# An encoder block on one core: the first phase's matmuls grouped by weight part, and the scalar work of the last product reordered

## The chip, the cores and the metric

The kernel runs on one core of a Trainium2 chip, in one launch. The metric is the device time in microseconds (us) of that core. The table of times has three runs of the kernel before, and one execution of it was also taken with the hardware profiler; its rows are what the prediction quotes. In those rows PE is the matmul engine, PEld its weight loads, DVE the vector engine, ACT the scalar engine, POOL the GpSimd engine, SP the engine that issues most transfers; a q behind an engine (ACTq, SPq) marks what its queue does, such as issuing a DMA. L324 is line 324 of the kernel before.

## The reference, cut to what matters

One encoder layer over 256 tokens of width 2048 in float32: a root-mean-square norm, one combined input projection, windowed and dilated attention, two gated branch projections, an output projection, a gated MLP with a convolution, and a gated per-token embedding, then a final norm. The change touches the first columns of the input projection and the very end:

```
h = rms_norm(x, attn_norm[i])
proj = h @ w_in[i]
...
gate_p = jax.nn.sigmoid(rms_norm(x, ple_norm[i]) @ w_ple_gate[i])
x = x + gate_p * (p[i] @ w_ple_proj[i])
...
return rms_norm(x, final_norm)
```

## The kernel before, in words

**Weights.** All weights come as one stream of 128x128 blocks in the order in which PE uses them (`_stream`). Blocks are loaded in tiles `raw` (six buffers, on SP's queue), mostly eight blocks each. `split_to` turns each such group, called a sub here, into a high part `whi` (ACT, L261) and a low part `wlo` (DVE, L262, which reads `whi`); both names have four buffers. The features are held in the same way: `hs` (named `mov` in the profile) has the high part of a feature chunk in its first 256 columns and the low part in the next 256. A product is high part times both halves (512 columns) plus low part times the first half (256 columns).

**The first phase.** Seven products (`FIRST = 7`, two keys and five queries of the windowed attention) run side by side while x and the weights arrive, for each of 16 feature chunks one block of each product, so 112 blocks. Their sums stand in seven banks (`firsts`, three named acc, two sp, two pt). The first piece of 16 blocks is cut in subs of 1, 2, 5, 4 and 4 blocks, and then each sub has eight: subs 0 to 16 belong to the first phase. The loop before emits, for each block, one matmul of the high part and at once one of the low part, in `block` (L324 and L325), as far as features and subs are there (`ready`, `_SUBS`).

**Between first phase and attention.** Two matmuls make the table of attention biases (L616, into the one-buffer bank `misc`), which DVE adds to the mask (`rows`, L618) and SP writes out. `tot` holds the squares of x summed over chunks; four calls sum it over partitions (L488, each shown as two matmuls, into `misc` again), DVE makes `rv` of it (L500), POOL raises it to the power -1/2 (L502), DVE writes it on diagonals (`rdg`, L510), and a matmul spreads it (L516, `misc` again). Each `first` is gathered from its bank by ACT (L464, tile t, two buffers) and DVE (L468, L470). Then comes the product of the values (L375 to L377, two acc banks), and after it the products of single heads (`eight`, L347 and L350), in which the high parts of eight blocks stand in a row and then eight low parts, each second sub the other way round, so that runs of 16 meet.

**The last product.** `last_gates` finishes the gate for the last 512 columns, first for the first 128 tokens (t = 0), then for the other 128 (t = 1), for these in two halves of 256 columns: the right half (side 1, whose rest of the product PE does first) and the left one (side 0). `gate_side` is tanh (ACT, L951), plus one times `ph` (L952), added to the residual (L953), squares with their sum (L954), times the last gain (L955). `last_root` makes the norm's factor (DVE L986, POOL L987), and `finish` scales and writes 128 tokens: the last 512 columns on DVE (L994, written by SP), the first 768 on ACT (L996, written on ACT's own queue, L997), the 768 between on DVE (L998, written by SP, L999).

**What sets the order.** The code is recorded, and a scheduler sets the order on each engine; instructions wrapped in `keep` stay in the order of the code among themselves. So an edit can move instructions that its lines do not name.

## Time and profile before

| | us |
|---|---|
| median of three runs | 1464.53 |
| lowest, highest | 1463.12, 1464.62 |
| the profiled execution, its own time | 1464.53 |
| its span in the profile | 1462.7 |
| what lies around the span | 1.83 |
| mean granted PE clock in it | 0.997 |

The profile's page gives busy time of each engine, the chain of work that ended last, and groups of instructions. A row of a timeline has the start, the time taken, the engine, the line, the tile written and the tiles read, and in brackets how long the engine sat idle before it and who ended that. A row of the chain has start, length and what it was; an x with a number joins that many equal pieces.

### The profile page before, as it was taken

How to read it: one execution, taken by the hardware profiler on the slowest of the kernel's cores; microseconds unless marked ns; L12 is line 12 of the kernel's file. 1: busy time of each engine (PE TensorE's matmuls, PEld its weight loads, DVE VectorE, ACT ScalarE, POOL GpSimd, SP SyncE). 2: the span in 40 equal slices, each digit the busy share in tenths (PEclk: the TensorE clock that was granted, in tenths of full speed). 3: DMA queues.
4: the chain of work that ended last, by engine and by line, in shares of the span. 5: the costliest groups of instructions: out<-in, count | busy, mean ns of one | idle time of the engine just before them, and what ended most of it. 6: DMA issues, size and time to landing. Idle time of an engine off the chain costs nothing.

```text
span 1462.7 us, 20616 instructions
## 1 busy us (share of the span) xinstructions
PE 1449.0 (99%) x7531; PEld 1242.1 (85%) x7531; DVE 1110.8 (76%) x1575; ACT 818.1 (56%) x1155; POOL 107.1 (7%) x178
## 2 busy tenths in 40 slices
PE   9999999999999999999999999999999999999997
PEld 8888888888888888788888888888888888888886
DVE  7687665656665668879888888897888876988665
ACT  7465444444444456666555555676555555666653
POOL 0000000001111100201111100102110100010000
PEclk9999999999999999999999999999999999999998
DMA  9754555558888967978888886989788875797652
GB/s 327 242 172 154 173 166 181 188 179 263 290 308 299 353 226 259 291 236 273 266 284 268 285 291 212 286 286 313 274 283 276 299 230 167 255 300 252 212 193 90
DMA packets 111729, 362.16 MB, mean 248 GB/s; under 512 B 12804, under 2 KB 17924, under 8 KB 111500
## 3 DMA queue, kind: packets, MB, share of 16 engines
q1 hardware_dynamic: 88908, 292.80, 59.3%
q0 software_dynamic: 20560, 63.71, 14.6%
q10 hardware_dynamic: 2160, 4.33, 1.0%
q8 instruction: 59, 0.97, 0.3%
q14 instruction: 42, 0.34, 0.1%
HBM read 324.06 MB, written 27.30 MB: 240 GB/s over the span
## 4 chain that ended last, share of the span: by engine, by line
PE 95%; issue 2%; DMA 1%; DVE 1%; ACT 0%; SPq 0%; POOLq 0%; POOL 0%; DVEq 0%; ACTq 0%
PE acc L347 29%; PE acc L350 15%; PE acc L375 9%; PE acc L377 9%; PE acc L376 9%; PE acc L427 6%; PE acc L428 6%; PE acc L426 6%; PE first L324 2%; PE first L325 1%; DMA x<-row 1%; PE pt L894 1%; PE pt L701 0%; DMA raw<-in_wts 0%; PE sp L660 0%
## 5 line engine op out<-in xcount | busy, mean ns | idle before, releaser
L262 DVE TENSOR_TENSOR wlo<-raw,whi 128x1024 fp32r<-128x1024 f32 (+2 forms) x556 | 649.7, 1180 | 192.0 <-ACT whi L261 186.0
L261 ACT ACTIVATE whi<-raw 128x1024 fp32r<-128x1024 f32 (+2 forms) x556 | 562.2, 1022 | 303.5 <-PE acc L377 188.7
L347 PE MATMUL acc<-mov,whi 128*128 128x512 f32 x1840 | 441.6, 391 | 0.0
L347 PEld LDWEIGHTS acc<-mov,whi 128*128 128x128 f32 x1840 | 337.8, 188 | 65.5
L350 PEld LDWEIGHTS acc<-mov,wlo 128*128 128x128 f32 x1840 | 237.3, 191 | 9.1 <-ACT mov L480 0.2
L350 PE MATMUL acc<-mov,wlo 128*128 128x256 f32 x1840 | 242.8, 283 | 0.0
L375 PE MATMUL acc<-whi,mov 128*128 128x512 f32 (+1 forms) x504 | 193.4, 384 | 0.0
L377 PE MATMUL acc<-whi,mov 128*128 128x512 f32 (+1 forms) x504 | 193.1, 383 | 0.0
L376 PE MATMUL acc<-wlo,mov 128*128 128x512 f32 (+1 forms) x504 | 193.0, 383 | 0.0
L464 ACT ACTIVATE t<-acc 128x256 f32<-128x256 f32 x115 | 43.9, 382 | 132.6 <-PE acc L347 132.6
L375 PEld LDWEIGHTS acc<-whi,mov 128*128 128x128 f32 x504 | 95.1, 189 | 18.6 <-DVE first L468 0.5
L377 PEld LDWEIGHTS acc<-whi,mov 128*128 128x128 f32 x504 | 95.1, 189 | 18.6
L376 PEld LDWEIGHTS acc<-wlo,mov 128*128 128x128 f32 x504 | 95.1, 189 | 18.3
L468 DVE TENSOR_TENSOR u<-acc,t 128x256 f32<-128x256 f32 x100 | 42.2, 422 | 72.9 <-ACT t L464 72.1
L426 PE MATMUL acc<-whi,act 128*128 128x512 f32 x207 | 80.8, 391 | 0.2 <-ACT whi L261 0.2
L427 PE MATMUL acc<-wlo,act 128*128 128x512 f32 x207 | 80.6, 389 | 0.0
L428 PE MATMUL acc<-whi,act 128*128 128x512 f32 x207 | 80.6, 389 | 0.0
L853 POOL DMA_DIRECT2D x<-row x36 | 31.0, 878 | 376.8 <-ACT row L858 255.2
L262 DVE TENSOR_TENSOR wlo<-sums,whi 128x1024 fp32r<-128x1024 f32 x37 | 45.1, 1219 | 10.3 <-ACT whi L261 10.3
L805 ACT ACTIVATE c<-c 128x256 f32<-128x256 f32 x44 | 18.3, 417 | 57.3 <-DVE c L804 57.3
L426 PEld LDWEIGHTS acc<-whi,act 128*128 128x128 f32 x207 | 38.8, 188 | 8.8 <-ACT whi L261 0.9
L427 PEld LDWEIGHTS acc<-wlo,act 128*128 128x128 f32 x207 | 38.9, 188 | 8.5 <-DVE wlo L262 0.2
(218 smaller groups left out, 1664.5 us busy)
## 6 DMA issues: line engine op xcount, KB each, us to landing
raw<-in_wts SPq DMA_DIRECT2D x477, 512.0 KB, 5.0
sums<-kept SPq DMA_DIRECT2D x37, 512.0 KB, 5.3
sums<-in_wts POOLq DMA_DIRECT2D x23, 512.0 KB, 7.7
kept<-sums POOLq DMA_DIRECT2D x23, 512.0 KB, 4.5
raw<-in_wts SPq DMA_DIRECT2D x39, 256.0 KB, 4.8
row<-in_wts POOLq DMA_DIRECT2D x37, 256.0 KB, 8.7
x<-row POOLq DMA_DIRECT2D x36, 256.0 KB, 7.9
two<-in_wts POOLq DMA_DIRECT2D x14, 512.0 KB, 8.2
```

What stands on the lines that cost most here:

```text
L261: nc.scalar.activation(hi, src, AF.Copy)
L262: ins = nc.vector.tensor_tensor(lo, src, hi.bitcast(F32), op=ALU.subtract)
L347: nc.tensor.matmul(acc, hi[:, k, :], m, start=(first and k == 0), stop=(last and k == SUB - 1), skip_group_check=True)
L350: nc.tensor.matmul(acc[:, T:], lo[:, k, :], m[:, :T], start=False, stop=False, skip_group_check=True)
L375: nc.tensor.matmul(acc, xh, hi, start=(k == 0), stop=False)
L376: nc.tensor.matmul(acc, xh, lo, start=False, stop=False)
L377: nc.tensor.matmul(acc, xl, hi, start=False, stop=(k == n - 1 - t * late))
L426: nc.tensor.matmul(acc, xh, hi, start=(e == 1), stop=False)
L427: nc.tensor.matmul(acc, xh, lo, start=False, stop=False)
L428: nc.tensor.matmul(acc, xl, hi, start=False, stop=(e == uses[name]))
L464: keep(nc.scalar.activation(t, acc[:, T:], AF.Copy, scale=scale))
L468: nc.vector.tensor_tensor(u, acc[:, :T], t, op=ALU.add)
```

## The change

In the first phase `firsts_to` takes the place of `block`: of each stretch within a sub it emits all high parts, then all low parts, and from sub 7 on each second sub the other way round. In `last_gates` the tanh of the right half is emitted ahead of `finish(0, ...)`, that of the left half stays behind it; all of them and the copies in `finish` are under `keep`. For t = 0 the middle 768 columns are scaled by ACT in place of DVE. The two multiplications by the last gain become one of 512 columns, behind the second `last_root`.

```diff
-    def block(acc, m, first, last, ahead=3):
...
-        nc.tensor.matmul(acc, hi[:, o, :], m, start=first, stop=False, skip_group_check=True)
-        nc.tensor.matmul(acc[:, T:], lo[:, o, :], m[:, :T], start=False, stop=last, skip_group_check=True)
...
+    def firsts_to(end):
+
+        while state["at"] < end:
+            a = state["at"]
+            s, o = _SUB_OF[a]
+            b = min(end, _SUBS[s][0] + _SUBS[s][1])
+            turned = s > 6 and s % 2 == 1
+            for low in (turned, not turned):
+                for c in range(a, b):
+                    k, e = divmod(c, FIRST)
+                    w, m = subs[s][low][:, o + c - a, :], hs[:, k, :]
+                    nc.tensor.matmul(firsts[e][:, T * low:], w, m[:, :2 * T - T * low], start=(k == 0 and not low),
+                                     stop=(k == KC - 1 and low != turned), skip_group_check=True)
+            state["at"] = b
+            if b == _SUBS[s][0] + _SUBS[s][1]:
+                del subs[s]
...
-        while state["at"] < min(FIRST * ready, _SUBS[state["sub"]][0]):
-            k, e = divmod(state["at"], FIRST)
-            block(firsts[e], hs[:, k, :], k == 0, k == KC - 1, ahead=0)
+        firsts_to(min(FIRST * ready, _SUBS[state["sub"]][0]))
...
-    def gate_side(n, t, acc, u, side, total):
+    def gate_side(n, t, u, side, total):
...
-        nc.scalar.activation(u[:, c], acc, AF.Tanh, scale=held["half"][:, t:t + 1])
...
-        return lambda: keep(nc.vector.tensor_tensor(u[:, c], r, held["lg"][:, n * W4:(n + 1) * W4][:, c], op=ALU.mult))
...
         keep(nc.vector.tensor_tensor(v[:, T:], other, v[:, T:], op=ALU.add))
+        keep(nc.scalar.activation(u[:, T:], v[:, T:], AF.Tanh, scale=held["half"][:, 1:2]))
         finish(0, r, tail)
         rest()
-        u, so = row(), held["so"][:, 1:]
-        gate_side(n, 1, v[:, T:], u, 1, held["side"])()
+        gate_side(n, 1, u, 1, held["side"])
         keep(nc.vector.tensor_tensor(so, so, held["side"], op=ALU.add))
-        scaled = gate_side(n, 1, acc[1][:, :T], u, 0, held["ss3"][:, 1, n:n + 1])
+        keep(nc.scalar.activation(u[:, :T], acc[1][:, :T], AF.Tanh, scale=held["half"][:, 1:2]))
+        gate_side(n, 1, u, 0, held["ss3"][:, 1, n:n + 1])
         r = last_root(1)
-        scaled()
+        keep(nc.vector.tensor_tensor(u, res[:, 1, n * W4:(n + 1) * W4], lg, op=ALU.mult))
         finish(1, r, u)
...
-        nc.scalar.activation(whole[:, :a], whole[:, :a], AF.Copy, scale=r)
+        keep(nc.scalar.activation(whole[:, :a], whole[:, :a], AF.Copy, scale=r))
         nc.scalar.dma_start(out[t][:, :a], whole[:, :a])
-        nc.vector.tensor_scalar(whole[:, a:b], whole[:, a:b], r, None, op0=ALU.mult)
+        if t == 0:
+            keep(nc.scalar.activation(whole[:, a:b], whole[:, a:b], AF.Copy, scale=r))
+        else:
+            nc.vector.tensor_scalar(whole[:, a:b], whole[:, a:b], r, None, op0=ALU.mult)
```

Three places show what becomes of the order. An x with a number joins equal rows; line numbers above 320 are larger by a few in the changed kernel.

**End of the first phase.** On PE, the last rows of the first phase and what follows, before:

```order
L324 MATMUL first<-mov,whi 128x512
L325 MATMUL first<-mov,wlo 128x256
L616 MATMUL misc<-ohr,tbs 20x512 x2
L375 MATMUL acc<-whi,mov 128x256
L376 MATMUL acc<-wlo,mov 128x256
L377 MATMUL acc<-whi,mov 128x256
```

The same place on PE in the changed kernel:

```order
L329 MATMUL first<-mov,whi 128x512 x16
L329 MATMUL first<-mov,wlo 128x256 x16
L329 MATMUL first<-mov,whi 128x512 x16
L329 MATMUL first<-mov,wlo 128x256 x8
L619 MATMUL misc<-ohr,tbs 20x512 x2
L493 MATMUL misc<-ones,tot 128x1 x4
L380 MATMUL acc<-whi,mov 128x256
L381 MATMUL acc<-wlo,mov 128x256
```

Single pairs have become runs of 16, and the sums of `tot` (L493, L488 before) have moved up from behind the values to right behind the bias matmuls. On DVE, the same stretch before, where `rows` reads what L616 made and `rv` what L488 made:

```order
L262 TENSOR_TENSOR wlo<-raw,whi 128x1024 x3
L468 TENSOR_TENSOR first<-first,t 128x256 x2
L470 SCALAR_TENSOR_TENSOR first<-first,t 128x256
L618 TENSOR_TENSOR rows<-misc,mk 20x512
L262 TENSOR_TENSOR wlo<-raw,whi 128x1024
L470 SCALAR_TENSOR_TENSOR first<-first,t 128x256 x4
L262 TENSOR_TENSOR wlo<-raw,whi 128x1024 x4
L500 TENSOR_SCALAR rv<-misc 128x4
L510 TENSOR_SCALAR rdg<-ident,rr 128x128 x2
```

And on DVE in the changed kernel:

```order
L262 TENSOR_TENSOR wlo<-raw,whi 128x1024 x4
L621 TENSOR_TENSOR rows<-misc,mk 20x512
L473 TENSOR_TENSOR first<-first,t 128x256 x2
L505 TENSOR_SCALAR rv<-misc 128x4
L475 SCALAR_TENSOR_TENSOR first<-first,t 128x256 x2
L515 TENSOR_SCALAR rdg<-ident,rr 128x128
L475 SCALAR_TENSOR_TENSOR first<-first,t 128x256 x2
L515 TENSOR_SCALAR rdg<-ident,rr 128x128
```

`rows` now stands behind a fourth split (that of sub 20), and `rv` and `rdg` have moved up by some splits.

**End of the values.** On PE, behind the product of the values, before:

```order
L377 MATMUL acc<-whi,mov 128x256
L347 MATMUL acc<-mov,whi 128x512 x8
L350 MATMUL acc<-mov,wlo 128x256 x4
L488 MATMUL misc<-ones,tot 128x1 x4
L350 MATMUL acc<-mov,wlo 128x256 x12
L516 MATMUL misc<-rdg,ones 128x256
L347 MATMUL acc<-mov,whi 128x512 x16
```

And there in the changed kernel:

```order
L382 MATMUL acc<-whi,mov 128x256
L352 MATMUL acc<-mov,whi 128x512 x8
L355 MATMUL acc<-mov,wlo 128x256 x16
L521 MATMUL misc<-rdg,ones 128x256
L352 MATMUL acc<-mov,whi 128x512 x16
```

The sums are gone from between the low parts; the spread of `rdg` stays where it was.

**The end of the program.** On ACT, from the last square of t = 0 on, before:

```order
L884 ACTIVATE row,marks<-x 128x512
L996 ACTIVATE x<-x,rr 128x768
L951 ACTIVATE row<-row,marks 128x256
L997 DMA out<-x 128x768
L951 ACTIVATE row<-acc,marks 128x256
L996 ACTIVATE x<-x,rr 128x768
L997 DMA out<-x 128x768
```

And on ACT in the changed kernel, where L967 and L972 are the two tanh and L1001 the scaling that came from DVE:

```order
L887 ACTIVATE row,marks<-x 128x512
L967 ACTIVATE row<-row,marks 128x256
L998 ACTIVATE x<-x,rr 128x768
L999 DMA out<-x 128x768
L1001 ACTIVATE x<-x,rr 128x768
L972 ACTIVATE row<-acc,marks 128x256
L998 ACTIVATE x<-x,rr 128x768
L999 DMA out<-x 128x768
```

The right half's tanh has gone ahead of the first scaling; the write of the first tokens and one more scaling now stand ahead of the left half's tanh.

More of the change, by code (lines that the diff above doesn't have):

```diff
@@ L316, in back @@
         state["back"] = j + 1
-    def block(acc, m, first, last, ahead=3):
-        b = state["at"]
-        s, o = _SUB_OF[b]
-        split_to(s + ahead)
-        hi, lo = subs[s]
-        nc.tensor.matmul(acc, hi[:, o, :], m, start=first, stop=False, skip_group_check=True)
-        nc.tensor.matmul(acc[:, T:], lo[:, o, :], m[:, :T], start=False, stop=last, skip_group_check=True)
-        state["at"] = b + 1
-        if o == _SUBS[s][1] - 1:
-            del subs[s]
+    def firsts_to(end):
[13 more added lines that the diff above has]
+                del subs[s]
     def product(i, moving, n):
@@ L954, in gate_side @@
         keep(nc.vector.scalar_tensor_tensor(row()[:, :T], r, 1.0, r, op0=ALU.mult, op1=ALU.mult, accum_out=total))
-        return lambda: keep(nc.vector.tensor_tensor(u[:, c], r, held["lg"][:, n * W4:(n + 1) * W4][:, c], op=ALU.mult))
     def last_gates(n, acc, rest):
-        v = row()
+        v, u, so, lg = row(), row(), held["so"][:, 1:], held["lg"][:, n * W4:(n + 1) * W4]
         keep(nc.scalar.activation(v[:, T:], acc[1][:, T:], AF.Copy))
```

## The prediction, made before the changed kernel ran

> **What bounds the kernel now.** I read the page's busy times and its chain first, then who PE waited for.

> ```profile
> PE 1449.0 (99%) x7531; PEld 1242.1 (85%) x7531; DVE 1110.8 (76%) x1575; ACT 818.1 (56%) x1155; POOL 107.1 (7%) x178
> PE 95%; issue 2%; DMA 1%; DVE 1%; ACT 0%; SPq 0%; POOLq 0%; POOL 0%; DVEq 0%; ACTq 0%
> ```

> ```profile
> PE misc L516 <- DVE rdg L510: 0.4, 1, 0.4
> ```

> PE is busy for 99% of the span and makes 95% of the chain; one of its few waits is that of the spread (L516) for `rdg`. So up to PE's last matmul, what PE saves or loses moves the end one to one, and what other engines save counts only where PE waits for them. Behind that matmul a chain over ACT, DVE and POOL sets the end. The sum has a front and a tail.

> **Front, the runs.** PE's rows in the first phase, and runs of the same shapes in the later products, from the chain:

> ```profile
> 12.22 1.66 PE L324 MATMUL first<-mov,whi 128*128 128x512 f32 x6 [0.53 <-ACT whi L261]
> ...
> 45.84 0.40 PE L324 MATMUL first<-mov,whi 128*128 128x512 f32 x1
> ...
> 46.28 0.63 PE L616 MATMUL misc<-ohr,tbs 32*20 32x512 f32 x2
> 46.85 0.39 PE L375 MATMUL acc<-whi,mov 128*128 128x256 f32 x1
> ```

> ```profile
> 657.85 0.43 PE misc L516 x2
> ...
> 661.11 3.65 PE acc L347 x16
> 664.76 1.91 PE acc L350 x16
> 666.67 3.65 PE acc L347 x16
> ```

> At 12.22 PE waits for sub 5, that is for its load and its split on ACT; whatever PE saves on the 16 blocks before is lost there. From there to the last pair at 45.84 stand 95 steps of one pair: 33.62/95 = 353.9 ns a pair, with hardly a gap. In runs 16 pairs take 666.67 - 661.11 = 5.56 us, 347.5 ns a pair. The new order gives runs of 8 and 16, the same shapes; I take 347.5. Over 96 pairs PE gains 96 x 6.4 ns = 0.61 us: the first phase ends at 45.58 in place of 46.19 (45.84 and one pair). Ends of this term: no gain and 0.61; more than the runs show has no row.

> [...]

> **Front, the sums.** The order shown ahead moves the sums of `tot` from behind the values to right behind the bias matmuls. Both write `misc`, which has one buffer; so the sums can't start before DVE's `rows` has read the bias product, and the values queue behind them on PE. On DVE `rows` now stands behind the split of sub 20. The rows of before for these, ACT and then DVE:

> ```profile
> 46.48 1.05 ACT L261 ACTIVATE whi<-raw 128x1024 fp32r<-128x1024 f32 x1
> ```

> ```profile
> 44.54 1.23 DVE L262 TENSOR_TENSOR wlo<-raw,whi 128x1024 fp32r<-128x1024 f32 x1 [1.60 <-ACT whi L261]
> 45.68 0.75 DVE L468 TENSOR_TENSOR first<-first,t 128x256 f32<-128x256 f32 x2
> ...
> 46.95 0.68 DVE L618 TENSOR_TENSOR rows<-misc,mk 20x512 f32<-20x512 f32 x1
> ```

> Sub 20's high part takes the buffer of sub 16's, free when PE's last run of high parts ends. That is eight low parts, 0.96 us (half of 1.91), before the phase ends: the last high part starts at 45.58 - 0.96 - 0.23 = 44.39 and ends 0.40 later, at 44.79. Then ACT 1.05, DVE's split 1.14 until its next row (44.54 to 45.68), `rows` 0.68, and four hand-overs between engines of about 0.04 (as from ACT's tanh at 1452.34 + 0.49 to DVE's row at 1452.87, below): 44.79 + 1.05 + 1.14 + 0.68 + 0.16 = 47.82. PE would have been free at 45.58 + 0.09 + 0.57 = 46.24 (46.19 to 46.28 and on to 46.85). So PE waits some 1.58 us. The sums then cost what they cost later before, and free what was there:

> ```profile
> 60.78 0.97 PE L488 MATMUL misc<-ones,tot 128*128 128x1 f32 x8
> 61.62 1.68 PE L350 MATMUL acc<-mov,wlo 128*128 128x256 f32 x12
> 63.72 0.67 PE L516 MATMUL misc<-rdg,ones 128*128 128x256 f32 x2 [0.42 <-DVE rdg L510]
> 64.04 4.02 PE L347 MATMUL acc<-mov,whi 128*128 128x512 f32 x16
> ```

> The sums hold PE for 0.84 (60.78 to 61.62), so the values start at 47.82 + 0.84 = 48.66 in place of 46.85: 1.81 late. Their banks are free by then: the two L473 behind `rows` take 0.75. The 0.84 is gone at 60.78. And the spread no longer waits: 12 low parts from 61.62 take 1.43, so PE was through at 63.05; alone the spread holds PE for 0.43 (row at 657.85), where it went on at 64.04, so 0.99 becomes 0.43: 0.56 saved. `rdg` is now made right behind the sums, with the whole product of the values between it and its matmul. Front: 1.81 - 0.84 - 0.56 = **+0.41 us**, the 0.61 of the runs included. Next in line are the scores, which waited for nothing before; their chain from the spread is the same, so nothing new is late. SP's bias write hangs on `rows`, which ends at nearly the same time as before (47.63 against 47.8). Ends of the wait: none at all (the front is then -0.61 - 0.56 = -1.17), or ACT's split starting only when the phase has ended, 0.96 later (+1.37). I take the value between, as each of its steps has a row.

> **Tail.** DVE, then ACT with one older case of a DMA issued from its queue, POOL, and PE's last row:

> ```profile
> 1449.85 0.69 DVE L944 TENSOR_TENSOR row<-x,end 128x512 f32<-128x512 f32 x1
> ...
> 1450.69 0.42 DVE L965 TENSOR_TENSOR row<-acc,row 128x256 f32<-128x256 f32 x1
> 1451.50 0.49 DVE L994 TENSOR_SCALAR row<-row,rr 128x512 f32<-128x512 f32 x1 [0.40 <-POOL rr L987]
> 1451.90 0.61 DVE L998 TENSOR_SCALAR x<-x,rr 128x768 f32<-128x768 f32 x1
> 1452.87 0.43 DVE L952 SCALAR_TENSOR_TENSOR row<-row,end 128x256 f32<-128x256 f32 x1 [0.35 <-ACT row L951]
> ...
> 1454.55 0.42 DVE L952 SCALAR_TENSOR_TENSOR row<-row,end 128x256 f32<-128x256 f32 x1
> ...
> 1455.92 0.16 DVE L986 TENSOR_TENSOR rv<-marks,sum 128x1 f32<-128x1 f32 x1
> 1456.00 0.42 DVE L955 TENSOR_TENSOR row<-x,end 128x256 f32<-128x256 f32 x1
> ```

> ```profile
> 1451.50 0.94 ACT L996 ACTIVATE x<-x,rr 128x768 f32<-128x768 f32 x1 [0.92 <-POOL rr L987]
> 1452.34 0.49 ACT L951 ACTIVATE row<-row,marks 128x256 f32<-128x256 f32 x1
> 1452.47 0.38 ACTq L997 DMA_DIRECT2D out<-x  x1
> 1453.43 0.47 ACT L951 ACTIVATE row<-acc,marks 128x256 f32<-128x256 f32 x1 [0.59 <-PE acc L399]
> ```

> ```profile
> 1236.20 0.33 ACTq L1064 DMA_DIRECT2D pr<-in_pt  x1
> 1236.63 0.63 ACT L261 ACTIVATE whi<-raw 128x512 fp32r<-128x512 f32 x1
> ```

> ```profile
> 1450.91 0.55 POOL L987 TENSOR_TENSOR rr<-rv,mhalf 128x1 f32<-128x1 f32 x1 [93.40 <-DVE rv L986]
> 1456.23 0.60 POOL L987 TENSOR_TENSOR rr<-rv,mhalf 128x1 f32<-128x1 f32 x1 [4.76 <-DVE rv L986]
> ```

> ```profile
> 1453.11 0.28 PE L399 MATMUL acc<-whi,mov 128*128 128x256 f32 x1
> ```

> In times of before: the right half's input is there at 1451.11 (L965), so its tanh runs on ACT from 1451.15, in the time in which ACT sat idle for POOL, and ends at 1451.64. The scaling of 768 columns can follow 0.40 to 0.45 after the tanh's start, at about 1451.55, 0.05 later than before. DVE has its 512 columns at 1451.50 and, without L998, starts the right half at 1451.90, not 1452.87: 0.97 earlier. But this is only half of the tail: the left half's first DVE row (1454.55 before) needs the left tanh, which now stands on ACT behind the first write and the moved scaling. The write is issued once the scaling is done: 1451.55 + 0.94 + 0.03 = 1452.52, and holds ACT's queue for 0.38, to 1452.90; an instruction behind such an issue started 0.10 after it (1236.53 to 1236.63), so the moved scaling runs from 1453.00, the tanh 0.84 behind it (as 1451.50 to 1452.34), from 1453.84 to 1454.31, and DVE goes on at 1454.35. PE's last matmul ends at 1453.39, so the tanh no longer waits for PE; ACT takes PE's place. DVE is ready earlier, at about 1453.3 (four steps of 0.46 from 1451.90, since the multiplication L955 is gone there). So the tail gains 1454.55 - 1454.35 = **0.20 us**, not 0.97. Were ACT not held by the issue, the tanh would again start at 1453.43 and the gain be 0.61; these are the ends.

> From 1454.35 on everything follows as before, but for the multiplication, now 512 columns (0.69, as L944) behind `rv`, where 256 stood (0.42). It runs while POOL makes the factor: `rv` to the end of POOL is 0.91 (1455.92 to 1456.83), `rv` and the multiplication 0.77, so it is hidden. If that cover fails, 0.27 (rival below). The middle write of the first tokens follows the moved scaling's end at 1453.94, not L998's at 1452.51:

> ```profile
> out<-x SPq DMA_DIRECT2D x2, 384.0 KB, 3.1
> ```

> At 1453.94 + 3.1 = 1457.04 it has landed before the last writes are issued (POOL's end, 1456.83 - 0.20, and a scaling of 0.61: 1457.24), so it costs nothing; without that cover it would share the engines with them for at most its delay of 1.43.

> **Sum.** +0.41 - 0.20 = +0.21 on the profiled execution's own 1464.53 (span 1462.7 and 1.83 around it): 1464.74, say 1464.7. The median of the three runs is the same 1464.53.

> **Rivals.**
> 1. *POOL is held by the multiplication.* L955 reads two SBUF tiles while POOL works; beside it POOL took 0.60, beside L965, which reads a bank and one tile, 0.55. If POOL has to wait until the longer multiplication ends, the factor comes 0.69 - 0.42 = 0.27 later: +0.48, 1465.0. For it: the 0.05. Against it: POOL started 0.19 before L955 ended and wasn't longer by that. [...]
> 2. *ACT isn't held by the issue*: -0.61 in the tail, +0.41 in front, -0.20: 1464.3. Against it: the 0.10 at 1236.53, and that the issue itself waits for the scaling.
> 3. *PE doesn't wait for `rows`*: -1.17 - 0.20 = -1.37, 1463.2. Against it: one buffer for both products.
> 4. *The change doesn't do what it says*: runs at the pace of pairs, +0.21 + 0.61 = +0.82, 1465.35. [...]
> 5. *Slower: the low runs starve.* A run of low parts of two subs takes 1.91 us, and needs the second sub's split at its start plus 0.96. Sub 9, in the first stretch that DVE filled with other work, has it from 20.24:

> ```profile
> 20.24 1.22 DVE L262 TENSOR_TENSOR wlo<-raw,whi 128x1024 fp32r<-128x1024 f32 x1
> ```

> It is there at 21.46; PE would want it at about 23.3 (12.22, four high runs of 1.83 and four low ones of 0.96). Slack 1.9 us: from a DVE that is later by more than that, each of the five such runs waits for up to one split, 5 x 1.23 = 6.15: 1470.9. Against it: the slack, and that later subs come earlier against their use.

> **How the numbers follow.** Chances: forecast 0.49, rival 1 0.22, rival 2 0.12, rival 3 0.08, rival 4 0.05, rival 5 0.03, and 0.01 for a gain that I don't see. All but the last two lie within 0.2% (2.9 us, about what a measurement of this kernel can tell from no change) of 1464.53: faster 0.01, same 0.96, slower 0.03. Range: the cases but rival 5 span 1463.2 to 1465.35; the later split adds up to 0.96 to the forecast (1465.7), and the runs of before lay up to 1.4 under their median. 1463.0 to 1466.0 holds them.

> **What would show it.** Right: the bias matmuls about 0.6 us earlier; a PE wait of about 1.6 us at the sums, put down to `rows`; no wait at the spread; the first head product behind the spread about 0.4 us later than 64.04; in the tail the left tanh some 0.4 us after PE's last matmul, right behind the moved scaling; POOL still about 0.6. Wrong: new PE waits for `wlo` between 12 and 46, POOL near 0.9, or other waits of PE after 80 us, where the orders are alike again.

## The result, and the profile after

| | kernel before | changed kernel |
|---|---|---|
| median, us (22 runs each) | 1464.32 | 1466.22 |
| lowest to highest, us | 1462.98 to 1465.65 | 1463.62 to 1468.92 |
| the profiled execution, us | 1464.53 | 1463.65 |
| its span, us | 1462.7 | 1461.9 |

The ratio is 1.0013, with an interval of 1.0007 to 1.0019: the changed kernel is 1.9 us slower, 0.22 us above the top of the range that was predicted. Yet the execution of it that was profiled is at the low end of its runs, below the median of the kernel before. A profile is one execution, and here that one lacks what most of the others have. So this section reads what every execution shares, and the experiments find the rest. One run of the changed kernel in those experiments took 3637.75 us, at full clock and for a reason that no record shows; it counts in the first median of their first table, but in no ratio.

PE of the changed kernel around the end of the first phase:

```profile
11.74 2.12 PE L329 MATMUL first<-mov,whi 128*128 128x512 f32 x8 [0.20 <-ACT whi L261]
...
44.32 1.11 PE L329 MATMUL first<-mov,wlo 128*128 128x256 f32 x8
45.36 0.63 PE L619 MATMUL misc<-ohr,tbs 32*20 32x512 f32 x2
47.48 1.08 PE L493 MATMUL misc<-ones,tot 128*128 128x1 f32 x8 [1.48 <-DVE rows L621]
48.42 0.36 PE L380 MATMUL acc<-whi,mov 128*128 128x256 f32 x1
...
63.77 0.59 PE L521 MATMUL misc<-rdg,ones 128*128 128x256 f32 x2
64.01 4.01 PE L352 MATMUL acc<-mov,whi 128*128 128x512 f32 x16
```

PE idles 1.48 us for `rows`, as forecast (1.58), and no longer waits at the spread. Sub 5 starts at 11.74, where it started at 12.22 before; that moves with the first loads, and was between 11.74 and 13.57 in the fourteen traces of this study. Counted from sub 5's start, the first head product comes after 64.01 - 11.74 = 52.27 us, and before after 64.04 - 12.22 = 51.82: the front is 0.45 later (forecast 0.41). Two misses cancel in this: the values start 2.05 us later (48.42 - 11.74 against 46.85 - 12.22; forecast 1.81), and 1.60 of it comes back before the head product (forecast 0.84 + 0.56 = 1.40).

The tail of the changed kernel, from ACT's tanh of the right half:

```profile
1450.38 0.51 ACT L967 ACTIVATE row<-row,marks 128x256 f32<-128x256 f32 x1 [0.56 <-DVE row L966]
...
1451.75 0.35 ACTq L999 DMA_DIRECT2D out<-x  x1
...
1452.14 0.94 ACT L1001 ACTIVATE x<-x,rr 128x768 f32<-128x768 f32 x1 [0.43 <-ACT x L998]
...
1452.99 0.46 ACT L972 ACTIVATE row<-acc,marks 128x256 f32<-128x256 f32 x1
1453.47 0.43 DVE L954 SCALAR_TENSOR_TENSOR row<-row,end 128x256 f32<-128x256 f32 x1 [0.79 <-ACT row L972]
...
1454.93 0.68 DVE L975 TENSOR_TENSOR row<-x,end 128x512 f32<-128x512 f32 x1
1455.16 0.87 POOL L989 TENSOR_TENSOR rr<-rv,mhalf 128x1 f32<-128x1 f32 x1 [4.46 <-DVE rv L988]
```

The left tanh stands right behind the moved scaling, which the write held back, as forecast. But POOL takes 0.87 us in place of 0.60: it ends at 1456.03, 0.42 behind the end of the 512-column multiplication (1455.61), as it ended 0.41 behind the shorter one before (1456.83 and 1456.42). From the start of PE's last matmul to the end of the span it is 9.53 us, before 9.58. So the tail gains 0.05, not 0.20.

This sums to +0.45 - 0.05 = +0.4 us. The median moved by 1.9. The first experiments ask where the other 1.5 us are.

### The profile page after: what moved, and what is told of

Read it like the earlier page. It is cut to its first block, busy times and chain, and to the rows that moved or that the text cites. A ratio compares the mean times of both kernels' runs of the same rounds, so it can differ in the third digit from the quotient of the medians.

```text
span 1461.9 us, 20619 instructions
## 1 busy us (share of the span) xinstructions
PE 1448.8 (99%) x7531; PEld 1242.9 (85%) x7531; DVE 1111.0 (76%) x1573; ACT 820.0 (56%) x1156; POOL 107.3 (7%) x178
## 4 chain that ended last, share of the span: by engine, by line
PE 97%; DMA 1%; ACT 1%; DVE 1%; issue 0%; SPq 0%; POOLq 0%; ACTq 0%; DVEq 0%
PE acc L352 29%; PE acc L355 15%; PE acc L380 9%; PE acc L382 9%; PE acc L381 9%; PE acc L432 7%; PE acc L433 6%; PE acc L431 6%; PE first L329 2%; DMA raw<-in_wts 1%; PE pt L897 1%; PE pt L704 0%; ACT whi L261 0%; PE misc L719 0%; PE sp L663 0%
## 5 line engine op out<-in xcount | busy, mean ns | idle before, releaser
L262 DVE TENSOR_TENSOR wlo<-raw,whi 128x1024 fp32r<-128x1024 f32 (+2 forms) x556 | 650.2, 1181 | 192.8 <-ACT whi L261 186.9
L261 ACT ACTIVATE whi<-raw 128x1024 fp32r<-128x1024 f32 (+2 forms) x556 | 562.7, 1023 | 302.4 <-PE acc L382 187.5
L469 ACT ACTIVATE t<-acc 128x256 f32<-128x256 f32 x115 | 43.7, 380 | 133.8 <-PE acc L352 133.7
L473 DVE TENSOR_TENSOR u<-acc,t 128x256 f32<-128x256 f32 x100 | 42.2, 422 | 73.3 <-ACT t L469 72.5
L262 DVE TENSOR_TENSOR wlo<-sums,whi 128x1024 fp32r<-128x1024 f32 x37 | 45.1, 1220 | 9.2 <-ACT whi L261 9.2
```

What stands on the lines that cost most here:

```text
L261: nc.scalar.activation(hi, src, AF.Copy)
L262: ins = nc.vector.tensor_tensor(lo, src, hi.bitcast(F32), op=ALU.subtract)
L469: keep(nc.scalar.activation(t, acc[:, T:], AF.Copy, scale=scale))
L473: nc.vector.tensor_tensor(u, acc[:, :T], t, op=ALU.add)
```

## The experiments

Ratios are against the kernel before, run on the same chip in the same session; its median there was between 1463.35 and 1463.80 us. Theories for the first four: A, the accumulating writes land later, so PE waits longer for them at its transposes near 630 us; B, sub 5 starts later; C, POOL is held longer in other executions than in the profiled one.

### The same kernels again, and each half of the change alone

The changed kernel again (no edit):

> The changed kernel once more, for its times beside the others of this call and for a second trace. Its median over 22 runs lay 1.9 us above the kernel before, while its one trace lay 0.8 us below that of before and shows +0.44 in the front and about 0 in the tail. Theory A (landing): the missing 1.5 us is PE's wait for the accumulating writes of the output projection to land (the transposes at 628 to 634 us, 0.6 us in the trace of after, 1.5 in that of before), which differs between executions; a trace whose time is near 1466.3 then shows 2.5 to 3.5 us there. Theory B (start): PE's first wait for a weight load (sub 5, at 11.7 us in after, 12.2 in before) ends later in most executions; such a trace shows sub 5 at 14 us or later. Theory C (tail): POOL's second factor, 0.87 in the trace, is held longer in most executions, by 1.5 us or more.

The first phase as changed, `last_gates`, `gate_side` and `finish` as before:

```diff
-    def gate_side(n, t, u, side, total):
+    def gate_side(n, t, acc, u, side, total):
...
-        keep(nc.scalar.activation(u[:, T:], v[:, T:], AF.Tanh, scale=held["half"][:, 1:2]))
```

> The grouped first phase with the end of the program as before. The forecast's front term alone is +0.4 us. Theory A or B: all of the 1.9 us is in the front's doing, so this kernel is 1.9 us over before (ratio 1.0013). Theory C: +0.4 (1.0003).

The tail as changed, the loop of the first phase as before:

```diff
-        firsts_to(min(FIRST * ready, _SUBS[state["sub"]][0]))
+        while state["at"] < min(FIRST * ready, _SUBS[state["sub"]][0]):
+            k, e = divmod(state["at"], FIRST)
+            block(firsts[e], hs[:, k, :], k == 0, k == KC - 1, ahead=0)
```

> The first phase as before with the new end of the program. By the two traces the tail is worth -0.04 us (DVE goes on 0.32 earlier, POOL's factor comes 0.26 later). Theories A and B: within 0.3 us of before (ratio 0.9998 to 1.0002). Theory C: +1.5 us (1.0010). In its trace POOL's second factor takes about 0.87 us beside the multiplication of 512 columns, as the rival that POOL is held had it.

The kernel before, once more (no edit):

> The kernel before once more, as a null: ratio 1.0000 within 0.0005. Its trace is a second execution of before. Theory A: its wait at the transposes of the output projection is again 1 to 2 us and differs from the first trace's 1.5 by as much as its time does; theory B: its sub 5 begins at 12.2 within 0.5 us and the time differs by that.

| | median, us | ratio | interval |
|---|---|---|---|
| changed kernel | 1465.95 | 1.0011 | 1.0002 to 1.0020 |
| front alone | 1465.94 | 1.0015 | 1.0006 to 1.0024 |
| tail alone | 1463.38 | 0.9996 | 0.9988 to 1.0005 |
| kernel before | 1463.18 | 0.9996 | 0.9988 to 1.0005 |

The whole loss is in the front; C falls. The wait at the transposes was 1.5 us in the first trace of before and between 0.3 and 1.1 in these four, without regard to the change, so A falls too. Sub 5 started at 12.63 and 12.12 in the two traces with the new front, at 12.22 and 11.94 in the others: B doesn't give 1.5 us either.

What gives it stands in the windows view. Its columns after the stretch are each engine's busy time (with instructions), the granted PE clock, DMA share and rate. First the changed kernel's first trace, then the new one:

```profile
46.00:50.00 4.00, 2.52 (x21) 2.52 (x22) 3.02 (x8) 1.55 (x5) 1.02 (x1) 1.00 0.32 78
50.00:54.00 4.00, 4.00 (x35) 4.00 (x35) 2.74 (x7) 1.44 (x2) 0.00 (x0) 1.00 0.95 343
```

```profile
46.00:50.00 4.00, 2.52 (x19) 1.86 (x19) 2.99 (x7) 1.74 (x5) 0.27 (x1) 1.00 0.09 20
50.00:54.00 4.00, 4.00 (x24) 4.00 (x22) 1.94 (x7) 1.22 (x4) 0.75 (x1) 0.57 0.95 320
54.00:58.00 4.00, 4.00 (x36) 4.00 (x35) 1.30 (x2) 2.00 (x2) 0.00 (x0) 1.00 0.49 177
```

PE is busy all the time from 50 to 54 in both, yet gets through 24 matmuls in place of 35, and the column of the clock says why: 0.57 in place of 1.00. The matmuls of the values in that trace:

```profile
48.37 1.08 PE L493 MATMUL misc<-ones,tot 128*128 128x1 f32 x8 [1.48 <-DVE rows L621]
...
50.23 0.28 PE L381 MATMUL acc<-wlo,mov 128*128 128x256 f32 x1
...
51.94 0.41 PE L381 MATMUL acc<-wlo,mov 128*128 128x256 f32 x1
52.15 0.41 PE L382 MATMUL acc<-whi,mov 128*128 128x256 f32 x1
...
54.35 0.28 PE L382 MATMUL acc<-whi,mov 128*128 128x256 f32 x1
54.47 0.28 PE L380 MATMUL acc<-whi,mov 128*128 128x256 f32 x1
```

The mean clock of each run, which is given for the runs without a profile too, shows roughly how often. One slow window lowers it by an estimated 0.5 x 3.413 / 1462 = 0.0012. The kernel before stood at 0.998 or 0.999 in 32 of 33 runs, the tail alone in 11 of 11; the changed kernel in 6 of 22 (median 1464.49), and lower in 16 (the twelve at 0.997: 1466.51). A single run's mean proves nothing, since the clock is half behind PE's last matmul, too, for a time that varies (the last 7.41 us of the span in the first trace of before, 5.21 in that of the changed kernel): the profiled execution of before, at 0.997, had no fall until then. The 2.0 us between those medians are more than the 1.49 of one window; what the rest is stays open.

### Taking the wait away, filling it, keeping it without the sums, the sums alone

The new theory: PE's quiet time (idle 1.48, and 0.94 of one-column sums behind it) lowers the clock of the next window. First, the sums kept behind the values:

```diff
-            nc.tensor.matmul(s[:, c:c + 1], total[:, tokens], ones[:, :1], start=True, stop=True)
+            keep(nc.tensor.matmul(s[:, c:c + 1], total[:, tokens], ones[:, :1], start=True, stop=True))
```

(and the last matmul of the values under `keep`, too)

> The changed kernel with its sums of tot kept behind the values, where they stood before; runs and tail as changed. Clock theory: in three traces of the changed front PE sat idle 1.48 us ahead of the sums; in the two where 1.31 and 1.48 us of it, and all sums, fell into one window of 3.413 us, the granted clock was 0.5 for the next 3.413 us (16 steps of the values at 0.213 in place of 0.120 us, 1.5 us). Without the wait no window is that quiet: clock 1.00 from 46 to 60 us, time 0.6 us under the kernel before (ratio 0.9996). Rival (the runs themselves, or a later start of sub 5, cost the 1.9 us): ratio 1.001 as for the changed kernel.

It was the slowest of all, 1466.48, ratio 1.0020 (1.0011 to 1.0029), and the expectation missed. PE, and then DVE, in its trace:

```profile
45.63 0.63 PE L619 MATMUL misc<-ohr,tbs 32*20 32x512 f32 x2
48.08 0.58 PE L380 MATMUL acc<-whi,mov 128*128 128x256 f32 x1 [1.82 <-DVE first L473]
```

```profile
45.88 1.23 DVE L262 TENSOR_TENSOR wlo<-raw,whi 128x1024 fp32r<-128x1024 f32 x1 [0.59 <-ACT whi L261]
47.02 0.67 DVE L621 TENSOR_TENSOR rows<-misc,mk 20x512 f32<-20x512 f32 x1
47.62 0.73 DVE L473 TENSOR_TENSOR first<-first,t 128x256 f32<-128x256 f32 x2
```

Without the sums PE still waits, and longer: the values need the banks of the first two products, which DVE gathers (L473) behind `rows`, and `rows` behind the split of sub 20. So the sums were only first in a queue that was late anyway. What makes it late should be the split of sub 20, ahead of the gathers on ACT and ahead of `rows` on DVE. ACT in the kernel before has the first two gathers (L464) ahead of that split (at 46.48); in this trace the split stands ahead of them (L469):

```profile
44.41 0.64 ACT L464 ACTIVATE t<-first 128x256 f32<-128x256 f32 x2
```

```profile
44.79 1.06 ACT L261 ACTIVATE whi<-raw 128x1024 fp32r<-128x1024 f32 x1 [0.75 <-PE first L329]
45.75 0.64 ACT L469 ACTIVATE t<-first 128x256 f32<-128x256 f32 x2
```

The clock fell here too (from 47.94 to 51.35), behind a window with 1.67 us of idling and 0.56 of bias matmuls.

Second, the wait filled with PE's own small matmuls (with L473 under `keep`, and the sums and the first matmul of the values, so that the orders on DVE and PE stay):

```diff
-    for e in range(2):
-        nc.tensor.matmul(b, tbs[:, e], ohr, start=(e == 0), stop=(e == 1))
+    for e in range(6):
+        nc.tensor.matmul(b, tbs[:, e % 2], ohr, start=(e % 2 == 0), stop=(e % 2 == 1))
```

> The changed kernel with the two bias matmuls done three times over, so that PE works through half of its idle 1.48 us; order on every other engine and the end of rows as in the changed kernel, so the values start when they did. Clock theory: at most 0.8 us idle and 0.94 us of one-column sums fall into a window; the clock stays at 1.00 in most executions, the time falls from 1.0013 to 1.0000 or 1.0003 of the kernel before. Rival (what the values lose they lose by the wait, the start or a later landing): nothing changes, 1.001 to 1.002.

1466.29, ratio 1.0018 (1.0009 to 1.0027); the clock fell in its trace and was low in 9 of 11 runs. So the filler did not help. The window that lowered the clock had 0.77 us of idling, 0.94 of one-column matmuls and 0.87 of bias matmuls; which of them count is asked below.

Third, the wait without the sums in it: they are kept behind the values, and one more bias matmul stands in their place (its product isn't used):

```diff
+    keep(nc.tensor.matmul(ps.tile([NH, 2 * T], F32, name='misc'), tbs[:, 0], ohr, start=True, stop=True))
```

> The sums behind the values, but one more bias matmul into misc ahead of the values (its product is not read), so PE idles 1.48 us for rows as in the changed kernel, without the one-column matmuls behind it. Values start some 0.95 us later than in the kernel before. Clock theory in which one-column matmuls count as hardly any activity: 1.48 us idle in a window of 3.413 is not enough, as at the flip in the kernel before (1.47 us idle, clock full): clock 1.00, about +0.5 to +0.95 us, ratio 1.0005. Clock theory in which only idle time counts: clock 0.5 for one window in most executions, ratio 1.0015.

1465.98, ratio 1.0016 (1.0007 to 1.0026), the clock low in 3 of 11 runs.

```profile
46.09 0.63 PE L619 MATMUL misc<-ohr,tbs 32*20 32x512 f32 x2
48.21 0.41 PE L623 MATMUL misc<-ohr,tbs 32*20 32x512 f32 x1 [1.48 <-DVE rows L621]
```

PE idled 1.48 again, and the clock stayed full in this trace. But here, too, a window's end, at 47.70, cut the wait, in 0.98 and 0.51, so the trace by itself says nothing about the sums. What speaks for their part is that 3 of 11 runs were low, where the changed kernel had 16 of 22. The front was 65.72 - 12.46 = 53.26, 1.44 later than before: I had set the price at 0.5 to 0.95 from the changed kernel's first trace, where sub 5 happened to start 0.48 earlier.

Fourth, the kernel before with its sums moved ahead of the values:

```diff
-    nc.sync.dma_start(hold, rows)
+    nc.sync.dma_start(hold, rows); held['tot'] = sums(tot, HALVES + TWINS)
```

> The kernel before with its sums moved ahead of the values, and nothing else. PE would be free at 46.85 and rows is there at 47.63, so PE idles about 0.8 us, then 0.94 of sums: values 1.6 us later, 0.84 and 0.56 given back: +0.2 us. Clock theory: 1.74 us of quiet are just about half a window, so the clock falls rarely or never: ratio 1.0001. Rival (the place of the sums by itself costs the 1.9 us): 1.001.

1465.05, ratio 1.0010 (1.0001 to 1.0018), the clock low in 6 of 11 runs. In its trace:

```profile
45.99 0.63 PE L616 MATMUL misc<-ohr,tbs 32*20 32x512 f32 x2
47.40 1.17 PE L488 MATMUL misc<-ones,tot 128*128 128x1 f32 x8 [0.77 <-DVE rows L618]
48.43 0.56 PE L375 MATMUL acc<-whi,mov 128*128 128x256 f32 x1
```

PE idled 0.77 and then did 1.0 us of one-column matmuls; the front was 1.70 later, of which 1.49 is the slow window and 0.21 the rest (expected: 0.2). So the place of the sums by itself carries most of the loss in half of the runs, without any runs of equal matmuls.

What fell into a window, and the clock of the window behind it, from the traces. "End" is the end of the program, where PE has done its last matmul:

| trace | window, us | idle | one-column sums | bias matmuls | together | clock after |
|---|---|---|---|---|---|---|
| changed, first | 46.97 to 50.38 | 0.51 | 0.94 | none | 1.45 | 1.0 |
| before, at the transposes | 632.66 to 636.08 | 1.46 | none | none | 1.46 | 1.0 |
| changed, first | 43.55 to 46.97 | 0.97 | none | 0.56 | 1.53 | 1.0 |
| wait without sums | 44.29 to 47.70 | 0.98 | none | 0.56 | 1.54 | 1.0 |
| front alone, end | 1452.21 to 1455.62 | 1.85 | none | none | 1.85 | 1.0 |
| before, end | 1451.86 to 1455.28 | 1.89 | none | none | 1.89 | 0.5 |
| changed, second, end | 1453.36 to 1456.77 | 1.90 | none | none | 1.90 | 0.5 |
| sums alone | 44.81 to 48.22 | 0.77 | 0.83 | 0.56 | 2.16 | 0.5 |
| sums behind | 44.52 to 47.93 | 1.67 | none | 0.56 | 2.24 | 0.5 |
| changed, second | 47.06 to 50.48 | 1.31 | 0.94 | none | 2.25 | 0.5 |
| filled | 47.78 to 51.19 | 0.77 | 0.94 | 0.87 | 2.58 | 0.5 |
| front alone | 45.92 to 49.33 | 1.48 | 0.94 | 0.47 | 2.89 | 0.5 |

Idle time and one-column sums alone don't sort these windows: 1.60 of them lowered the clock in the trace of the sums alone, and 1.85 left it full at the end of the front alone. With the bias matmuls counted, too, they sort: up to 1.85 us the clock stayed full, from 1.89 on it fell. If windows at the end count like those in the front, the border lies between these two, a little over half of a window. By the same table the one-column sums count as quiet for the most part: without them the sums alone would stand at 1.33 with all bias matmuls counted, below windows that left the clock full, and to pass 1.85 it takes 0.52 of their 0.83.

### Taking away the cause

If the split of sub 20 ahead of the gathers is the cause, it suffices to keep the splits of subs 19 and 20 behind them, with `rows` behind the first two gathers:

```diff
-            nc.scalar.activation(hi, src, AF.Copy)
+            (keep if s in (19, 20) else lambda i: i)(nc.scalar.activation(hi, src, AF.Copy))
...
-            if _BLOCKS[a][0] in ("w_out", "w_ffn_down"):
+            if _BLOCKS[a][0] in ("w_out", "w_ffn_down") or s in (19, 20):
...
-                               keep)
+                               keep); i == 1 and rows_out()
```

> The changed kernel with the splits of subs 19 and 20 kept behind the gathers of the first two banks and rows, on ACT and on DVE, and rows behind the two gathers' DVE rows; the sums then fall behind the values as in the kernel before, the runs stay. Theory (the runs let ACT split sub 20 before the gathers; DVE takes that split ahead of the gathers and rows; PE then idles and its clock falls for a window): the first gathers are done at about 46.1, so the values start 0.6 to 0.75 us earlier than in the kernel before, the clock is 1.00 from 46 to 60 us in every execution, ratio 0.9996. Rival (runs alone cost something that the windows only accompany): ratio 1.001 or more.

Then the sums in the middle of the values as well:

```diff
-            rms([(START, 6), (START, 12)], lambda: sums(tot, HALVES + TWINS), 0, 4)
+            rms([(FIRST, 8), (START, 12)], lambda: sums(tot, HALVES + TWINS), 0, 4)
```

> As the kernel with the splits behind the gathers, and the sums of tot in the middle of the values instead of behind them, so that rdg is ready when the spread comes. Theory: no wait at the sums (rows is long read), none at the spread (0.42 less), values 0.6 to 0.75 us earlier than in the kernel before, the clock full: 1.0 to 1.1 us under the kernel before, ratio 0.9993. If one-column matmuls between full ones were enough to lower the clock, 1.5 us more.

And with that the last multiplication in two parts again:

```diff
+        keep(nc.vector.tensor_tensor(u[:, T:], res[:, 1, n * W4 + T:(n + 1) * W4], lg[:, T:], op=ALU.mult))
...
-        keep(nc.vector.tensor_tensor(u, res[:, 1, n * W4:(n + 1) * W4], lg, op=ALU.mult))
+        keep(nc.vector.tensor_tensor(u[:, :T], res[:, 1, n * W4:n * W4 + T], lg[:, :T], op=ALU.mult))
```

> As the kernel with the sums in the middle of the values, and in the tail the last multiplication again in two parts of 256 columns, the right half's right behind its own squares and only the left half's behind the second rv. Theory (POOL is held by the 512-column multiplication, 0.87 us in the changed kernel against 0.60): POOL takes about 0.60 again and the end comes 0.25 us earlier than with one multiplication; 1.3 us under the kernel before, ratio 0.9991. Rival (POOL's time does not hang on it): POOL 0.87, ratio as without this edit.

| | median, us | ratio | interval | clock at 0.998 or more |
|---|---|---|---|---|
| kernel before, same session | 1463.35 | | | 26 of 27 |
| splits behind the gathers | 1463.44 | 0.9997 | 0.9988 to 1.0006 | 10 of 11 |
| sums in the middle, too | 1463.16 | 0.9994 | 0.9985 to 1.0003 | 11 of 11 |
| two multiplications, too | 1462.38 | 0.9992 | 0.9983 to 1.0001 | 11 of 11 |

PE in the trace of the first of them, and its clock:

```profile
45.95 0.64 PE L619 MATMUL misc<-ohr,tbs 32*20 32x512 f32 x2
46.51 0.39 PE L380 MATMUL acc<-whi,mov 128*128 128x256 f32 x1
```

```profile
46.00:50.00 4.00, 4.00 (x32) 3.55 (x32) 3.04 (x8) 2.77 (x7) 0.00 (x0) 1.00 0.31 88
50.00:54.00 4.00, 4.00 (x36) 4.00 (x35) 3.83 (x4) 2.95 (x3) 0.00 (x0) 1.00 0.98 330
```

The values follow the bias matmuls without a gap, and the front is 51.38 (from 12.33 to 63.70), 0.44 shorter than in the first trace of before. With the sums in the middle it is 51.20, where PE waited 0.24 for a low part at 18.18, and in the third kernel, where no low part came late, 50.72. So the grouping gains its 0.44 once nothing idles behind it, as against that trace; the second trace of before, with a faster first phase (see below), had 51.28. Each interval reaches 1, so that none of these is shown faster by its times; their traces show where they gain. The tail of the third, DVE and POOL:

```profile
1454.37 0.42 DVE L976 TENSOR_TENSOR row<-x,end 128x256 f32<-128x256 f32 x1
1454.60 0.60 POOL L990 TENSOR_TENSOR rr<-rv,mhalf 128x1 f32<-128x1 f32 x1 [4.46 <-DVE rv L989]
```

POOL is back at 0.60, and from PE's last matmul to the end it is 9.28 us, against 9.54 in the two others. That settles the tail: the 512-column multiplication held POOL for 0.27.

### What counts as quiet

Last, in the kernel with the splits behind the gathers, ten bias matmuls in place of two, so that PE never idles but works narrowly:

```diff
-    for e in range(2):
+    for e in range(10):
```

> The kernel with the splits behind the gathers, and its two bias matmuls done five times over (10 matmuls of 20x512 from 32 rows, the same product): PE works without a gap, but through some 2.4 us of narrow matmuls. They cost 8 times 0.23 = 1.9 us, so the head products start 1.9 us later than without them. If a window's activity is the time in which PE has work, the clock stays at 1.00 and the ratio is 0.9997 + 0.0013 = 1.001. If narrow matmuls count as hardly any activity, as the kernel with two thirds of the wait filled by them suggests, the clock is 0.5 for one window of 3.413 us in most executions, 1.5 us more: 1.002.

1464.75, ratio 1.0010 (1.0001 to 1.0019); the clock stayed full in the trace and in 9 of 11 runs. So the ten matmuls cost their own time and, in most runs, no more. This doesn't show that they count as work: the window with most of them, 46.91 to 50.32, has 1.67 us of them and no idling, and 1.67 is below the 1.85 of idling that left the clock full. By the table they count as quiet at least in part: the sums alone had 1.60 without its 0.56 of them, and need 0.25 of that to pass 1.85. If they counted fully, a window that holds nearly all of this kernel's 2.42 us would lower the clock, and with evenly spread windows that would be about 7 of 11 runs, an estimate with the border at 1.87: (3.41 - 2.42 + 2 x (2.42 - 1.87))/3.41 = 0.61. It was 2. How much such a matmul counts stays open.

## Why the prediction was right and wrong

- **The runs, -0.61.** Right in kind. From sub 5's first matmul to the start of the last low part it took 33.86 or 33.87 us in three traces of the old order and 33.40 to 33.42 in eight of ten traces of the new (33.30 and 33.90 in the others): 0.45. One trace of the kernel before took 33.32, so that the old order has a second pace, and the gain isn't there in each execution.
- **The wait, 1.58.** Right: 1.48. Half right in its cause: "one buffer for both products" is what PE waits for, but with the sums out of the way it waited 1.82 for the gathers behind the same DVE queue. "Their banks are free by then" held only because the sums waited as well.
- **The spread, 0.56.** Right: no wait. That the profiled front came to +0.45 for a forecast of +0.41 is in part luck, as two misses of 0.2 cancel in it.
- **The step that failed** is the sum of the front, where "the values start at 48.66 in place of 46.85" and all behind them was taken to run as before. The wait was priced by its length alone. What it leaves behind, a window of 3.413 us at half clock, costs 1.49 more, in some 16 of 22 runs by their mean clock: 0.45 + 1.49 - 0.05 = 1.89, and 1.90 was measured. So close a match is luck, as the runs with and without the fall lie 2.0 apart and not 1.49. No rival had it, and the range's top was found from the wait's length ("0.96 later") and not from what a wait does. In the front of the profile of before nothing showed it: its longest wait behind the start, 1.46, left the clock full. Only behind PE's last matmul is there a fall, at 1455.28, where it costs nothing.
- **The tail, -0.20.** The order was right (left tanh behind write and moved scaling; its DVE row 0.32 earlier, 1.12 behind the start of PE's last matmul in place of 1.44). Rival 1, with a chance of 0.22, was the true one: POOL 0.27 later, so that 0.05 is left. The prediction's "four steps of 0.46 from 1451.90" come to 1453.74 and not to 1453.3; nothing hangs on it, as DVE sat idle 0.79 us for the left tanh. POOL's factor took 0.87 beside the multiplication of 512 columns, and 0.60 beside that of 256, before and in the kernel with two multiplications.
- **Rivals 4 and 5** (no pace gained, low runs starving): the pace was gained as said, and no trace of the changed kernel shows a wait for `wlo` in the first phase. One trace with the same runs does, that of the sums in the middle: 0.24 at 18.18.

## What to carry to other kernels

Price a new wait of the matmul engine twice, by its length and by what it does to the clock behind it: here a wait of 0.77 to 1.82 us, with the small matmuls beside it, brought 2.16 to 2.89 us of quiet into one window of 3.413 us, and the slow window behind it cost another 1.49 us. Look at the granted clock of many runs before trusting one profile, since the one profiled execution may be the lucky one: the same wait of 1.48 us was cut by a window's end in the changed kernel's first trace, 0.97 and 0.51, which left the clock full, and not so in its second, 0.17 and 1.31. And where grouping sets a buffer free earlier, see which queue its next user now stands ahead in.

## What was not expected of the hardware

- A clock that fell to half behind a window with 1.89 us of idling, at the end of the program, while 1.85 left it full there. No single wait behind sub 5's start was longer than 1.82 in the front, and the clock fell there in five of these traces, each time for one window of 3.413 us (50.48 to 53.89, 47.94 to 51.35).
- One-column matmuls, with 0.12 us from one to the next, count like idling for the most part by the table of windows (0.52 of 0.83 us at least, with all bias matmuls counted); 512-column ones on 32 rows count so at least in part (0.25 of 0.56).
- The alternating pairs of the old order ran at 353.9 ns a pair in three traces, and at (33.32 - 0.24)/95 = 348.2 in a fourth, of the same program (0.24 from a pair's high part to its low part).
